# Gate units as 512-column pairs, with another release of sums, other slots and another last half group

## The chip, the cores and the metric

The kernel runs on one core of one Trainium2 chip. The metric is the device time of one execution in microseconds. Each comparison takes the median of several runs; the kernel before has 1409.77 us as the median of three runs (1408.69 to 1409.82).

## The reference

One decoder block with batch 1, 256 positions, width 2048, everything in float32. Cut to what matters:

```python
mod = silu(c) @ w_ada + b_ada                      # 2048 -> 6*2048: sh1, sc1, g1, sh2, sc2, g2
h = rms_norm(x, norm_mix_g) * (1 + sc1) + sh1
u, q, k, v, ga, gb = split(h @ w_in)               # 1024 | 3 x 1024 | 2048 | 2048
y_ssm = s5_branch(u, ...)                          # a scan over the positions, gelu, times sigmoid(y @ w_glu + b_glu)
y_att = moba_attention(q, k, v, rel_bias)          # 8 heads of 128, causal, bias by distance
merged = sigmoid(ga) * (y_ssm @ w_proj_ssm) + sigmoid(gb) * (y_att @ w_proj_attn)
x = x + g1 * (merged @ w_out)
h2 = rms_norm(x, norm_mlp_g) * (1 + sc2) + sh2
x = x + g2 * (square(relu(h2 @ w_ff1)) @ w_ff2)    # 2048 -> 8192 -> 2048
return rms_norm(x, norm_final_g)
```

## The kernel before

**Products.** A float32 product is made of three products of shorter numbers. Each weight tile is loaded as 128 x 1024 floats (512 KB, tile `wraw`, seven buffers) by SyncE's queue; ScalarE casts it to its high part (`whi`, L137) and VectorE subtracts that to get the low part (`wlo`, L139), four buffers each. The activations are split the same way (`ah`, `al`; `mh` in the second half). TensorE adds up whi·xh, whi·xl and wlo·xh in PSUM. There are five PSUM banks for the large products (`bank`) and three for others (`aux`). `stream` runs over the 128-row tiles of a weight column block, issues load, cast and subtraction ahead of time, and calls `step` after each tile.

**Forms of the product.** `gemm_t` (L174 to L176) keeps a block of 1024 weight columns in four banks and multiplies 128x128 weight blocks by 256 columns of activations, three matmuls a block: 16 tiles x 8 blocks x 3 = 384 for a unit. `gemm_w` (L202, L204) takes half as many weight columns and lets the high weight block meet high and low activations side by side in `ahl`, 512 columns; one matmul of 256 columns for the low part follows. The left 256 columns of a bank then hold one part of the result and the right 256 the other, which an evacuation has to add. ff1 works in this form. `gemm_n` and `gemm_h` (L232 to L234, L271 to L273) hold the activations as the stationary side and let 512 weight columns stream, three matmuls of 512.

**Stages.** In order: the modulation sums that the first norm needs; the units of w_in (u, q, k, v in `qkvu`; the gate columns 4096 in pieces, whose last adds are L986; then three full gate units at columns 5120, 6144 and 7168); projections and w_glu; w_out; the second norm; then ff1 and ff2 in eight groups of 1024 hidden columns; the final norm and the stores.

**Work beside it.** `step` pops jobs off lanes at a rate for each weight tile: a job is popped when the rate has added up to 1.
- Lane `ada`: the rest of the modulation, 176 loads of 512 KB with one multiply-and-sum on VectorE each (L327). Its rate is set by stage: R3 and then RS0, RS1, RS2 through w_in and the gates, RPA in the projections, RWO in w_out.
- Lanes `ssm` and `tab` build the tables of the scan. The table products (`cc`, `tt`, L581 to L583) end in TensorE's `rk` matmuls (L651), whose results VectorE takes in L657.
- Lane `m`: in gate unit 1 (columns 5120) and ahead of it the attention, from the unit's middle on (`to_ssm`) the scan.
- POOL's queue carries the hops of u between partitions (`hop_in`, L757, 32 transfers; `hop_out`) and the loads of the bias table `tz` (`bias_load`, L457, eight transfers).

**The attention.** For a head: scores `sco` (L705, L706), bias added from `tz` (L708, L709), maxima, exponentials (L713, L714), scaling (L716, L717), transposes `ptr` (L724) with a copy (L725), then `pav` (L732, L733) with a copy to `yatt` (L735). The probabilities and their transposes lie in `asc`, a part of the tile `ga`: blocks 8 to 13, one half for even and one for odd heads. Gate unit 1 has the blocks 8 to 15 of `ga` as its destination.

**Slots.** `slot` gives a named place in SBUF that several tiles hold one after the other; a tile waits until the holder before it is done. `T` and `S5` are two of them.

**Order.** The program is written in stages, but a scheduler orders the instructions of each engine by priorities and modelled times; `hot` and `high_priority` move work ahead.

## Time and profile before

| what | value |
|---|---|
| median of three runs | 1409.77 us |
| the profiled execution | 1411.44 us |
| its span | 1409.3 us |
| mean granted TensorE clock | 0.991 |
| TensorE busy | 1371.2 us |
| VectorE busy | 1056.0 us |
| ScalarE busy | 706.4 us |
| moved by DMA | 353.19 MB |

The page is of one execution, 1411.44 us; the 2.1 us between that and the span lie outside what the profiler dates. Matmuls are pipelined: one that the trace shows as 0.28 us long starts 0.12 us after the one before it, so their cost is read from start to start. Line numbers are those of the kernel before. In the changed kernel a line stands one lower than before between the constants and `homes`, and 24 higher from the new function on.

### The profile page before, as it was taken

The page shows a single profiled execution, that of the slowest core. Times are in us where ns is not written, and L with a number is a line of the kernel's source. Part 1 is how long each engine was busy: PE and PEld are TensorE (multiplying, and loading weights), DVE is VectorE, ACT ScalarE, POOL GpSimd, SP SyncE. Part 2 cuts the span into 40 slices and gives each one's busy share as a digit, 9 for nine tenths or more (in the row PEclk, how much of TensorE's full clock was granted, in tenths as well). Part 3 has the DMA queues.
Part 4 walks back from the last instruction along what each step waited for, and adds up shares of the span by engine and source line. Part 5 has one row for each costly group of instructions (what it writes and reads, how often), then busy time and mean ns, then how long its engine had stood idle before and what let it go on. Part 6 is the DMA issues. An engine that isn't in the chain of part 4 may idle for free.

```text
span 1409.3 us, 23394 instructions
## 1 busy us (share of the span) xinstructions
PE 1371.2 (97%) x9258; PEld 1221.7 (87%) x9258; DVE 1056.0 (75%) x1502; ACT 706.4 (50%) x937; POOL 40.9 (3%) x94
## 2 busy tenths in 40 slices
PE   7889999999999999999999999999999999999996
PEld 6789899899999999988788888888888888888885
DVE  5788989986799888978877776767676555655676
ACT  4454343366454853455655564545463544635444
POOL 1000000320000300000000000000000000000000
PEclk9999999999999999999999999999999999999998
DMA  9999987597457988887687677777767556565551
GB/s 349 373 382 363 318 293 233 159 299 241 149 186 257 316 294 297 296 335 276 229 298 269 209 262 239 254 247 268 264 220 263 186 188 195 176 203 191 183 203 60
DMA packets 113293, 353.19 MB, mean 251 GB/s; under 512 B 12080, under 2 KB 12096, under 8 KB 113056
## 3 DMA queue, kind: packets, MB, share of 16 engines
q1 hardware_dynamic: 110384, 347.13, 70.6%
q0 software_dynamic: 2800, 4.58, 1.1%
q8 instruction: 72, 1.18, 0.3%
q14 instruction: 37, 0.30, 0.1%
HBM read 347.27 MB, written 2.29 MB: 248 GB/s over the span
## 4 chain that ended last, share of the span: by engine, by line
PE 86%; DMA 6%; DVE 5%; ACT 1%; issue 1%; SPq 0%; DVEq 0%; ACTq 0%
PE pw L202 14%; PE pn L271 10%; PE pn L273 10%; PE pn L272 10%; PE pt L174 9%; PE pt L176 9%; PE pt L175 9%; PE pw L204 7%; DMA wraw<-in_w_in_dram 3%; DVE wlo L139 2%; DVE wraw L327 1%; PE pn L233 1%; PE pn L234 1%; PE pn L232 1%; DMA wraw<-in_wat_dram 1%
## 5 line engine op out<-in xcount | busy, mean ns | idle before, releaser
L137 ACT CAST whi<-wraw 128x1024 fp32r<-128x1024 f32 x443 | 461.9, 1052 | 553.5 <-PE pn L272 177.1
L139 DVE TENSOR_TENSOR wlo<-wraw,whi 128x1024 fp32r<-128x1024 f32 x443 | 538.3, 1223 | 255.8 <-ACT whi L137 252.9
L202 PE MATMUL pw<-mh,whi 128*128 128x512 f32 x896 | 311.5, 396 | 0.2 <-DVE part L1260 0.2
L174 PE MATMUL pt<-ah,whi 128*128 128x256 f32 x896 | 251.4, 288 | 7.2 <-ACT whi L137 5.1
L175 PE MATMUL pt<-ah,whi 128*128 128x256 f32 x896 | 250.3, 285 | 0.0
L204 PE MATMUL pw<-mh,wlo 128*128 128x256 f32 x896 | 243.0, 280 | 1.0 <-DVE wlo L139 1.0
L176 PE MATMUL pt<-ah,wlo 128*128 128x256 f32 x896 | 237.7, 286 | 2.8 <-DVE wlo L139 2.5
L327 DVE SCALAR_TENSOR_TENSOR wraw<-wraw,cb 128x1024 f32<-128x1024 f32 x176 | 213.6, 1220 | 0.0
L272 PE MATMUL pn<-whi,ff 128*128 128x512 f32 x512 | 199.3, 389 | 0.0
L271 PE MATMUL pn<-whi,ff 128*128 128x512 f32 x512 | 198.6, 390 | 0.0
L202 PEld LDWEIGHTS pw<-mh,whi 128*128 128x128 f32 x896 | 165.4, 188 | 36.3 <-issue 0.5
L273 PE MATMUL pn<-wlo,ff 128*128 128x512 f32 x512 | 185.4, 389 | 0.0
L174 PEld LDWEIGHTS pt<-ah,whi 128*128 128x128 f32 x896 | 172.1, 193 | 10.8 <-ACT whi L137 6.8
L204 PEld LDWEIGHTS pw<-mh,wlo 128*128 128x128 f32 x896 | 168.8, 188 | 5.5 <-DVE wlo L139 1.4
L175 PEld LDWEIGHTS pt<-ah,whi 128*128 128x128 f32 x896 | 172.6, 193 | 0.7 <-DVE ah L139 0.2
L176 PEld LDWEIGHTS pt<-ah,wlo 128*128 128x128 f32 x896 | 164.7, 193 | 4.8 <-DVE wlo L139 4.4
L271 PEld LDWEIGHTS pn<-whi,ff 128*128 128x128 f32 x512 | 96.1, 188 | 20.0 <-issue 0.2
L273 PEld LDWEIGHTS pn<-wlo,ff 128*128 128x128 f32 x512 | 96.1, 188 | 20.1
L272 PEld LDWEIGHTS pn<-whi,ff 128*128 128x128 f32 x512 | 96.1, 188 | 19.6
L1294 DVE TENSOR_TENSOR y<-y,pn 128x512 f32<-128x512 f32 x48 | 30.9, 683 | 14.8 <-PE pn L273 14.8
L271 PE MATMUL pn<-whi,mh 128*128 128x512 f32 x96 | 37.7, 392 | 0.0
L272 PE MATMUL pn<-whi,mh 128*128 128x512 f32 x96 | 37.4, 390 | 0.0
(400 smaller groups left out, 1658.1 us busy)
## 6 DMA issues: line engine op xcount, KB each, us to landing
wraw<-in_w_ff_dram SPq DMA_DIRECT2D x256, 512.0 KB, 4.7
wraw<-in_wat_dram SPq DMA_DIRECT2D x176, 512.0 KB, 5.5
wraw<-in_w_in_dram SPq DMA_DIRECT2D x128, 512.0 KB, 5.3
wraw<-in_w_out_dram SPq DMA_DIRECT2D x32, 512.0 KB, 6.3
wraw<-in_wan_dram SPq DMA_DIRECT2D x16, 512.0 KB, 8.7
wraw<-in_w_proj_attn_dram SPq DMA_DIRECT2D x16, 512.0 KB, 6.2
wraw<-in_w_proj_ssm_dram SPq DMA_DIRECT2D x16, 512.0 KB, 5.8
wraw<-in_w_glu_dram SPq DMA_DIRECT2D x8, 512.0 KB, 5.0
```

What stands on the lines that cost most here:

```text
L137: h = self.nc.scalar.copy(hi, src)
L139: s = self.nc.vector.tensor_sub(lo, src, hi.bitcast(F32))
L174: nc.tensor.matmul(o, hi[:, c], xh[:, kx, :], start=st, stop=False, skip_group_check=True)
L175: nc.tensor.matmul(o, hi[:, c], xl[:, kx, :], start=False, stop=False, skip_group_check=True)
L176: self.mm = nc.tensor.matmul(o, lo[:, c], xh[:, kx, :], start=False, stop=sp, skip_group_check=True)
L202: nc.tensor.matmul(banks[b], hi[:, c], x2[:, k0 + k].rearrange("p h s -> p (h s)"), start=i + k == 0, stop=False, skip_group_check=True)
L204: self.mm = nc.tensor.matmul(banks[b][:, 0:S], lo[:, c], x2[:, k0 + k, 0, :], start=False, stop=i == n - 1 and k == 1, skip_group_check=True)
L271: nc.tensor.matmul(o, xh[:, kx, tk], hi[:, c], start=q == 0, stop=False)
L272: nc.tensor.matmul(o, xl[:, kx, tk], hi[:, c], start=False, stop=False)
L273: self.mm = last = nc.tensor.matmul(o, xh[:, kx, tk], lo[:, c], start=False, stop=q == n - 1)
L327: v.scalar_tensor_tensor(w, w, 1.0, self.cb[:, (i % 2) * 1024:(i % 2 + 1) * 1024], op0=OP.mult, op1=OP.mult, accum_out=pc[:, i:i + 1])
L1294: v.tensor_add(d, d, banks[b])
```

## The change

- The three full gate units are done by `gemm_w`, in two halves of 512 columns each, with `ahl`. After each half, four times: ScalarE copies one 256-column part of a bank, and VectorE adds the other. The attention's lane is flushed when the first half of unit 1 has been issued, ahead of that half's evacuation.
- R3 goes from .5 to .25 and RS1 from .25 to .1; RPA from .65 to .85 and RWO from .45 to .65. All 176 sums are still made.
- `bias_load` stands ahead of `hop_in`. `tz`, `sri` and `yl` move from slot T to S5; `yatt` and `sg` from S5 to T.
- The second column half of the last ff2 group is done by the new `gemm_e`: row block 0 of the output while the eight tiles stream in, then row block 1 from the tiles held, as one piece of 512 columns and two of 256. Four of the tiles are held in the slot `AHL`. The final norm of row block 0 is issued between the two. Two of the four stores of row block 1 are issued by ScalarE's queue.

```diff
-R3 = .5
+R3 = .25
...
-RS1 = .25
+RS1 = .1
...
-RPA = .65
-RWO = .45
+RPA = .85
+RWO = .65
...
-TF = 3
...
-            n = 2 if tag in ("VT", "QT") else 1
+            n = {"VT": 2, "QT": 2, "AHL": 4}.get(tag, 1)
...
+    def gemm_e(self, src, kts, c0, xh, xl, homes, koff):
+        nc = self.nc
+        n = len(kts)
+        def dot(o, t, c, i, kt, hi, lo):
+            tk, kx = slice(t * P, (t + 1) * P), kt - koff
+            nc.tensor.matmul(o, xh[:, kx, tk], hi[:, c], start=i == 0, stop=False)
+            nc.tensor.matmul(o, xl[:, kx, tk], hi[:, c], start=False, stop=False)
+            self.mm = nc.tensor.matmul(o, xh[:, kx, tk], lo[:, c], start=False, stop=i == n - 1)
+        first = [(self.bank("pe0"), slice(0, 512)), (self.aux("pe1"), slice(512, 1024))]
+        held = []
+        for i, unit in enumerate(self.stream(src, kts, c0, homes)):
+            held.append((i,) + unit)
+            for o, c in first:
+                dot(o, 0, c, *held[-1])
+        yield first
+        then = []
+        for name, c in (("pe2", slice(0, 512)), ("pe3", slice(512, 768)), ("pe4", slice(768, 1024))):
+            o = (self.aux(name) if name == "pe3" else self.bank(name))[:, 0:c.stop - c.start]
+            for u in held:
+                dot(o, 1, c, *u)
+            then.append((o, c))
+        yield then
...
     def bias_load(self):
-        self.tz = self.slot("T", [P, H, S], name="tz")
+        self.tz = self.slot("S5", [P, H, S], name="tz")
...
-        self.sri = self.slot("T", [P, 2, 2, 512], name="sri")
+        self.sri = self.slot("S5", [P, 2, 2, 512], name="sri")
...
-        self.hop_in()
         self.flush("ssm")
...
+        self.hop_in()
...
-        self.yatt = self.slot("S5", [P, 8, S], name="yatt")
+        self.yatt = self.slot("T", [P, 8, S], name="yatt")
         gb = self.slot("S1", [P, KT, S], name="gb")
...
             dst, c0 = ((ga, 4096), (ga, 5120), (gb, 6144), (gb, 7168))[i]
-            banks = self.gemm_t(win, range(KT), c0, self.ah, self.al, mid=to_ssm if i == 1 else None)
-            for b in range(4):
-                nc.scalar.copy(dst[:, (i % 2) * 8 + 2 * b:(i % 2) * 8 + 2 * b + 2, :],
-                               banks[b].rearrange("p (k s) -> p k s", s=S))
+            for half in range(2):
+                banks = self.gemm_w(win, range(KT), c0 + 512 * half, self.ahl)
+                if (i, half) == (1, 0):
+                    to_ssm()
+                for b in range(4):
+                    d = dst[:, (i % 2) * 8 + 4 * half + b]
+                    with self.hot():
+                        nc.scalar.copy(d, banks[b][:, S:2 * S])
+                        v.tensor_add(d, d, banks[b][:, 0:S])
...
-        yl = self.slot("T", [P, 8, S], F32R, name="yl")
+        yl = self.slot("S5", [P, 8, S], F32R, name="yl")
...
-        sg = self.slot("S5", [P, 4, 2, S], name="sg")
+        sg = self.slot("T", [P, 4, 2, S], name="sg")
...
-        fq = self.col("fq", 8)
+        fq = self.col("fq", 9)
...
         def final(t):
...
-                v.reduce_sum(fs, fq[:, 4 * t:4 * t + 4], axis=AX.X)
+                v.reduce_sum(fs, fq[:, 4 * t:4 * t + 4 + t], axis=AX.X)
...
                 for c in (2, 0, 3, 1):
...
-                    nc.sync.dma_start(self.out[0, t * P:(t + 1) * P, cc], o)
+                    q = nc.sync if t == 0 or c in (0, 2) else nc.scalar
+                    q.dma_start(self.out[0, t * P:(t + 1) * P, cc], o)
+        def last2(t, o, c, q, keep=None):
+            keep = keep or (lambda ins: ins)
+            d = acc[:, t, c]
+            with self.hot():
+                keep(v.tensor_mul(d, o, g2b[:, c]))
+                keep(v.tensor_add(x1[:, t, c], x1[:, t, c], d))
+                nc.scalar.activation(d, x1[:, t, c], AF.Square, accum_out=fq[:, q:q + 1])
...
         def ff2(g):
             f = ffs.pop(g)
-            for cg in range(2):
-                banks = self.gemm_n(w2, range(8 * g, 8 * g + 8), cg * 1024, f[:, 0], f[:, 1], koff=8 * g,
-                                    tail=TF if g == 7 and cg else 1)
+            for cg in range(1 if g == 7 else 2):
+                banks = self.gemm_n(w2, range(8 * g, 8 * g + 8), cg * 1024, f[:, 0], f[:, 1], koff=8 * g)
...
-                        with self.hot():
-                            v.tensor_mul(d, banks[b], g2b[:, c])
-                            v.tensor_add(x1[:, t, c], x1[:, t, c], d)
-                            nc.scalar.activation(d, x1[:, t, c], AF.Square,
-                                                 accum_out=fq[:, t * 4 + cg * 2 + b % 2:t * 4 + cg * 2 + b % 2 + 1])
-                        if cg == 0:
-                            v.tensor_mul(x1[:, t, c], x1[:, t, c], gfb[:, c])
-                        elif b % 2:
-                            final(t)
+                        last2(t, banks[b], c, t * 4 + b % 2)
+                        v.tensor_mul(x1[:, t, c], x1[:, t, c], gfb[:, c])
+            if g == 7:
+                halves = self.gemm_e(w2, range(56, 64), 1024, f[:, 0], f[:, 1], self.homes(4, ("AHL",)), 56)
+                for t in range(2):
+                    for j, (o, c) in enumerate(next(halves)):
+                        last2(t, o, slice(1024 + c.start, 1024 + c.stop), t * 4 + 2 + j, self.pin if t else None)
+                    final(t)
```

**TensorE, first half of gate unit 1 and the boundary behind it.** `pt` and `pw` are the banks of gate units (`pt` by gemm_t, `pw` by gemm_w; pw_3369 to pw_3372 are the first half's four banks, pw_3754 the first bank of the second half), `pav`, `sco` and `ptr` the attention. Before, at a head late in unit 1:

```order
L174 MATMUL pt_3398<-ah,whi 128x256
L175 MATMUL pt_3398<-ah,whi 128x256
L176 MATMUL pt_3398<-ah,wlo 128x256
L732 MATMUL pav<-ga,v 128x256
L733 MATMUL pav<-ga,v 128x128
L705 MATMUL sco<-qk 128x128
L706 MATMUL sco<-qk 128x256
L724 MATMUL ptr<-ident,ga 128x128 x3
L174 MATMUL pt_3398<-ah,whi 128x256
L175 MATMUL pt_3398<-ah,whi 128x256
L176 MATMUL pt_3398<-ah,wlo 128x256
L174 MATMUL pt_3399<-ah,whi 128x256
```

After, where heads 3 to 6 stand:

```order
L201 MATMUL pw_3754<-ah,whi 128x512
L203 MATMUL pw_3754<-ah,wlo 128x256
L756 MATMUL pav<-ga,v 128x256
L757 MATMUL pav<-ga,v 128x128
L729 MATMUL sco<-qk 128x128
L730 MATMUL sco<-qk 128x256
L748 MATMUL ptr<-ident,ga 128x128 x3
L756 MATMUL pav<-ga,v 128x256
L757 MATMUL pav<-ga,v 128x128
L729 MATMUL sco<-qk 128x128
L730 MATMUL sco<-qk 128x256
L748 MATMUL ptr<-ident,ga 128x128 x3
```

Before, the heads had two dozen gate matmuls between them; now `pav`, `sco` and `ptr` of several heads follow one another.

**ScalarE at the same place.** Copies from the banks into `ga` are L1093 before and L1122 after. Before:

```order
L716 ACTIVATE ga<-ga,ast 128x128
L717 ACTIVATE ga<-ga,ast 128x256
L725 COPY ga<-ptr 128x384
L137 CAST whi<-wraw 128x1024
L1093 COPY ga<-pt_3399 128x512
L1093 COPY ga<-pt_3396 128x512
L735 COPY yatt<-pav 128x256
L1093 COPY ga<-pt_3397 128x512
L725 COPY ga<-ptr 128x384
L735 COPY yatt<-pav 128x256
L1093 COPY ga<-pt_3398 128x512
```

After:

```order
L740 ACTIVATE ga<-ga,ast 128x128
L741 ACTIVATE ga<-ga,ast 128x256
L1122 COPY ga<-pw_3369 128x256
L737 ACTIVATE ga,ast<-ga,ast 128x128
L749 COPY ga<-ptr 128x384
L738 ACTIVATE ga,ast<-ga,ast 128x256
L740 ACTIVATE ga<-ga,ast 128x128
L741 ACTIVATE ga<-ga,ast 128x256
L1122 COPY ga<-pw_3370 128x256
L1122 COPY ga<-pw_3371 128x256
L759 COPY yatt<-pav 128x256
L1122 COPY ga<-pw_3372 128x256
```

The first bank's copy of the changed kernel stands between the scalings of the heads (L740, L741), the next ones behind the last scaling.

**VectorE ahead of the last write of cc**, which the rk matmuls need. L986 (after: L1010) is the last add of the gate columns 4096, L583 (L607) the writes of the table product, L327 (L351) a sum. Before, the rows from the last L986 to the first writes of cc:

```order
L986 TENSOR_TENSOR ga<-gp,pt_2306 128x512
L139 TENSOR_TENSOR wlo<-wraw,whi 128x1024
L327 SCALAR_TENSOR_TENSOR wraw,pc<-wraw,cb 128x1024
L888 TENSOR_TENSOR A_114<-pcs,cols 128x4
L582 TENSOR_TENSOR tt<-bp,AB 128x1024
L583 TENSOR_TENSOR tt<-bp,AB 128x1024
L139 TENSOR_TENSOR wlo<-wraw,whi 128x1024
L889 SCALAR_TENSOR_TENSOR A_114<-A_114,cols 128x4
L583 TENSOR_TENSOR bp<-tt 128x32x32
L581 TENSOR_TENSOR tt<-cc,AB 128x512 x2
L139 TENSOR_TENSOR wlo<-wraw,whi 128x1024
L327 SCALAR_TENSOR_TENSOR wraw,pc<-wraw,cb 128x1024
```

After, from the last L1010 to the last write of cc:

```order
L1010 TENSOR_TENSOR ga<-gp,pt_2300 128x512
L138 TENSOR_TENSOR wlo<-wraw,whi 128x1024
L351 SCALAR_TENSOR_TENSOR wraw,pc<-wraw,cb 128x1024
L606 TENSOR_TENSOR cc<-tt 128x32x16
L138 TENSOR_TENSOR wlo<-wraw,whi 128x1024
L606 TENSOR_TENSOR tt<-cc,AB 128x512
L607 TENSOR_TENSOR tt<-cc,AB 128x512
L607 TENSOR_TENSOR cc<-tt 128x32x16
L605 TENSOR_TENSOR tt<-cc,AB 128x1024 x2
L138 TENSOR_TENSOR wlo<-wraw,whi 128x1024
L606 TENSOR_TENSOR cc<-tt 128x32x32
L606 TENSOR_TENSOR tt<-cc,AB 128x1024
```

Two sums before and one after stand between the two; the products with bp (L582, L583) that stood behind the last gate add are now ahead of it.

## The prediction

> **What bounds the kernel now.** I read the page first: busy shares, the granted clock and the shares of the chain that ended last.
>
> ```profile
> PE 1371.2 (97%) x9258; PEld 1221.7 (87%) x9258; DVE 1056.0 (75%) x1502; ACT 706.4 (50%) x937; POOL 40.9 (3%) x94
> ...
> PEclk9999999999999999999999999999999999999998
> ...
> PE 86%; DMA 6%; DVE 5%; ACT 1%; issue 1%; SPq 0%; DVEq 0%; ACTq 0%
> ...
> L139 DVE TENSOR_TENSOR wlo<-wraw,whi 128x1024 fp32r<-128x1024 f32 x443 | 538.3, 1223 | 255.8 <-ACT whi L137 252.9
> ...
> L327 DVE SCALAR_TENSOR_TENSOR wraw<-wraw,cb 128x1024 f32<-128x1024 f32 x176 | 213.6, 1220 | 0.0
> ```
>
> TensorE is busy in 97% of the span and holds 86% of the chain. A change pays only if it takes away matmul time, one of TensorE's few idle stretches, or time behind the last matmul. VectorE's two costliest groups are the lo split (1.22 us a tile) and the modulation sum (176 of 1.22 us); each sum also needs its own 512 KB load. Next came busy time by stage: gate units beside the attention (332 to 382), the later gate units (to 477), projections and w_out (to 680), the first ff1 units (to 787).
>
> ```profile
> 332.00:382.00 50.00, 50.00 (x498) 48.97 (x497) 31.67 (x58) 28.40 (x59) 0.00 (x0) 1.00 0.50 157
> 382.00:477.00 95.00, 95.00 (x1163) 93.60 (x1162) 90.30 (x125) 52.90 (x66) 12.34 (x26) 1.00 0.69 228
> 477.00:680.00 203.00, 201.83 (x1360) 186.94 (x1358) 171.08 (x228) 104.71 (x129) 3.04 (x7) 1.00 0.84 306
> ```
>
> The columns are length, then busy time of PE, weight load, DVE, ACT and POOL, clock, DMA share and GB/s. In the gate units TensorE never stops and the clock is full, so matmul time saved there is saved at the end. From 382 to 477 VectorE is busy for 90.30 of 95 us, from 477 to 680 for 171.08 of 203 with the DMA engines at 0.84: that stage has little room.
>
> **The gate units.** The start-to-start spacing of matmuls, first in a gate unit, then in an ff1 unit, which already has the form that the change gives to the gates:
>
> ```profile
> 384.72 0.28 PE L175 MATMUL pt<-ah,whi 128*128 128x256 f32 x1
> ...
> 385.92 0.28 PE L176 MATMUL pt<-ah,wlo 128*128 128x256 f32 x1
> ```
>
> ```profile
> 1266.67 0.40 PE L202 MATMUL pw<-mh,whi 128*128 128x512 f32 x1
> ...
> 1309.69 0.40 PE L202 MATMUL pw<-mh,whi 128*128 128x512 f32 x1
> ```
>
> ```profile
> 1267.00:1310.00 43.00, 42.77 (x124) 22.85 (x124) 1.00 0.58 189
> ```
>
> Ten starts take 1.20 us in the gate: 0.120 for 256 columns, 0.360 for a triple. In ff1 the 512-column matmuls (124 records in that window, the last row, counted for L202 alone) go from 1266.67 to 1309.69: 43.02/123 = 0.350 for a pair of 512 and 256 columns. A unit has 128 triples or pairs: 46.1 us now, 44.8 after, −1.3 each and **−3.9 us** for three. The Trainium skill, page "TensorE: Matmul & The Clock Gate", section "Back-to-back issue gap", gives N/2.4 + 2.5 ns as the isolated gap: 327.5 for the triple, 325 for the pair, −1.0 us in all; the measured 0.120 is not its 0.109, so I keep the rows, and its result stands among the rivals.
>
> The evacuation changes too: now four ScalarE copies of 512 columns a unit, after it eight copies of 256 and eight VectorE adds, as ff1 has them.
>
> ```profile
> L1259 ACT COPY fr<-pw x32: 359/370/376, 1021.0 to 1312.1; 128x256 f32<-128x256 f32 x32
> L1260 DVE TENSOR_TENSOR fr<-fr,pw x32: 411/414/417, 1023.4 to 1313.4; 128x256 f32<-128x256 f32 x32
> L1093 ACT COPY ga<-pt x4: 581/589/606, 363.4 to 369.7; 128x512 f32<-128x512 f32 x4
> ```
>
> ScalarE gains work of 8 × 0.37 − 4 × 0.59 = 0.6 us a unit, hidden in its half-idle time. VectorE gains 24 × 0.414 = 9.9 us; four or five sums (5 to 6 us) leave the same stage, so the net is some +4.5 us against the 23 that are free from 332 to 477. I take 0; if that cover were gone, at most those 4.5 us.
>
> **The early sums.** Fewer are released before the scan tables' first matmuls (rk). What that clears is TensorE's longest stop after the start:
>
> ```profile
> 236.02 0.69 DVE L986 TENSOR_TENSOR ga<-gp,pt 128x512 f32<-128x512 f32 x1
> ...
> 255.54 0.28 PE L175 MATMUL pt<-ah,whi 128*128 128x256 f32 x1
> ...
> 257.16 1.22 DVE L583 TENSOR_TENSOR cc<-tt 128x1024 f32<-128x1024 f32 x1
> ...
> 258.42 1.66 ACT L641 COPY tt<-cmp 128x512 f32<-128x512 f32 x3 [6.15 <-DVE cc L583]
> 259.09 0.48 PE L651 MATMUL rk<-cc,tt 64*64 64x64 f32 x4 [3.27 <-ACT tt L641]
> ```
>
> TensorE's last matmul before the stop starts at 255.54; the next waits 3.27 us for copies that wait for the last write of cc. VectorE needs 22.4 us from the last add at 236.02 to the end of that write (258.38). In the changed order there stand four lo splits, one sum and about 10 us of table work, some 16 us: 6.4 earlier, more than the stop is long. Rk keeps its place among the matmuls. The clock behind it:
>
> ```profile
> 254.68:258.09 3.41, 1.14 (x10) 0.94 (x8) 3.34 (x4) 0.00 (x0) 0.00 (x0) 1.00 0.00 0
> 258.09:264.92 6.83, 5.83 (x94) 5.49 (x96) 6.05 (x9) 4.26 (x7) 0.00 (x0) 0.50 0.57 176
> ```
>
> After the idle stretch the granted clock was 0.50 for 6.83 us. At half speed that costs at most half, 3.4 us; about 1 us of it was idle, so I estimate 2.7. Stop and clock: **−6.1 us**. Ends: 0 (something else ends the wait) and −6.7. What is late next is the lo split that feeds the following unit, which also comes earlier.
>
> The sums reappear later: by the order, 58 instead of 43 stand in the stage from 477 to 680. VectorE's 171.1 us become 171.1 + 15 × 1.22 = 189.4 of 203 (93%), and 15 more loads of 0.5 MB on 62 MB raise the DMA share of 0.84 to about 0.94. On average it fits; local pile-ups in 14 us of slack I put at **+1.0 us**. Ends: 0 and +9 (half of the 18.3 us uncovered). Behind 680 the order has 5 instead of 8 sums up to the first lo part of ff1, where TensorE waits now:
>
> ```profile
> PE pw L204 <- DVE wlo L139: 1.0, 1, 1.0
> ```
>
> This wait goes: **−0.9 us** (0 to −1.0).
>
> **Bias table and slots.** The eight loads of the bias table go ahead of the 32 hops of u on POOL's queue, which means that POOL issues them before the gather instead of behind it.
>
> ```profile
> L457 POOL DMA_DIRECT2D tz<-scr x8: 532/532/556, 288.4 to 293.1; - x8
> ```
>
> They take 8 × 0.53 = 4.3 us of that queue, and I take 0: the slot comes free with the scan tables, ahead of the hops, so they fit in front. If they didn't, u and the scan behind it would come up to 4.3 us later, under gate matmuls that fill TensorE. The attention moves up by one unit.
>
> **A new wait at unit 1's middle.** The attention's scratch lies in ga, blocks 8 to 13. Before, unit 1 (c0 = 5120) wrote ga behind the whole unit, when the heads were done. Now its first half is evacuated into blocks 8 to 11 after half a unit, so those copies wait for the heads; and with five banks the second half has one bank until then. The changed TensorE order shows it: heads 3 to 6 stand with almost no gate matmuls between them. One head now:
>
> ```profile
> 326.80 0.60 PE L706 MATMUL sco<-qk 128*128 128x256 f32 x2
> ...
> 327.23 0.49 PE L724 MATMUL ptr<-ident,ga 128*128 128x128 f32 x3
> ...
> 327.76 0.48 ACT L725 COPY ga<-ptr 128x384 f32<-128x384 f32 x1 [0.61 <-PE ptr L724]
> ...
> 329.31 0.40 ACT L713 ACTIVATE ga<-ga,ast 128x128 f32<-128x128 f32 x1
> 329.62 0.19 ACT L713 ACTIVATION_READ_ACCUMULATOR ga<-ga,ast 128x1 f32 x1
> 329.71 0.50 ACT L714 ACTIVATE ga<-ga,ast 128x256 f32<-128x256 f32 x1
> ...
> 331.08 0.49 ACT L717 ACTIVATE ga<-ga,ast 128x256 f32<-128x256 f32 x1
> 331.48 0.35 ACT L735 COPY yatt<-pav 128x256 f32<-128x256 f32 x1
> ```
>
> The loop of one head: scaling on ScalarE (0.3 + 0.5 with overlap), transposes on TensorE (0.49), copy (0.48), the next head's exponentials (0.4 + 0.5 and their read-outs, about 1.0), the output copy (0.35): 0.8 + 0.49 + 0.48 + 1.0 + 0.35 = 3.1, with hand-overs 3.2 us. The stretch has three and a half such loops, about 11.1 us, and holds by the rows above some 5.8 us of matmuls (about 1.6 a head and a few gate pairs): 5.3 idle, and 0.8 more until the last copy frees a bank. **+6.1 us.** Ends: +3 (loops overlap better) and +10 (the clock drops as well). VectorE and ScalarE go on meanwhile, but they can't bank the time: the weight buffers are four deep.
>
> **The new end.** The last half group of ff2 (eight weight tiles) is done row block 0 first, and then row block 1, whose last columns are a 256-wide piece. One bank's pass costs 3 × 8 matmuls; the extra split costs 48 × 0.118 − 24 × 0.2265 = +0.23 us by the spacing above, and perhaps 0.3 of waiting for a lo part. Behind the last matmul now:
>
> ```profile
> 1397.94 0.39 PE L273 MATMUL pn<-wlo,ff 128*128 128x512 f32 x1
> ...
> 1401.06 4.50 SPq L1281 DMA_DIRECT2D out_dram<-x  x8
> 1401.61 0.15 DVE L1272 TENSOR_REDUCE fs<-fq 128x1 f32<-128x4 f32 x1
> ...
> 1402.99 1.41 DVE L1280 SCALAR_TENSOR_TENSOR x<-x,r31s,gfb 128x512 f32<-128x512 f32 x2
> ```
>
> The reduction at 1401.61 stands behind row block 0's scaling, and all eight stores are issued on one queue until 1405.56. With row block 0 gone, the 256-wide tail (add, square) ends near 1399.9, the root takes 1.4, the two scalings 1.4, and four stores on two queues end near 1403.5: −2.1, and with the +0.5 above **−1.6 us** (−0.5 to −2.5).
>
> **Sum.** −3.9 − 6.1 + 1.0 − 0.9 + 6.1 − 1.6 = −5.4 us. The profiled execution took 1411.44 us (span 1409.3 and 2.1 around it), 1.7 above the median of 1409.77; from the median the forecast is 1409.8 − 5.4 = 1404.4, I say 1404.5. Less than 0.2% (2.8 us, 1407.0 to 1412.6) can't be told from no change.
>
> **The rivals.**
> - *A: the clock halves in the attention stretch.* That the clock falls without one long gap is seen here:
>
> ```profile
> 155.69:159.10 3.41, 1.97 (x10) 1.09 (x8) 2.56 (x5) 0.93 (x1) 0.00 (x0) 1.00 1.02 410
> 159.10:165.93 6.83, 5.27 (x24) 5.28 (x25) 6.83 (x10) 3.14 (x3) 0.00 (x0) 0.50 0.91 326
> ```
>
> ```profile
> 742.80:753.00 10.20, 9.16 (x53) 7.80 (x52) 7.47 (x12) 3.39 (x5) 0.00 (x0) 1.00 0.92 323
> ```
>
> 1.44 us idle out of 3.41, in pieces, and 0.50 for the next 6.83 us. The new stretch idles 5.3 of 11.1, some 1.6 per 3.41, just there. Price about +4: 1408.5. Against it: the last row, from 742.80 on, has 1.04 us idle in its first third and full clock to its end. The Trainium skill, page "TensorE: Matmul & The Clock Gate", section "Why this matters for your kernels", asks for no idle gap above some 3 us; by that rule no single gap here is long enough and the clock stays, which the rows above contradict, so they weigh more. Chance 0.22.
> - *B, slower: VectorE and the loads become the bound between 477 and 680.* 93% busy leaves 14 us, and TensorE needs each lo part in time. It decides once more than 6 of the 18.3 us are uncovered; half uncovered gives +9 in place of +1: 1412.5 to 1413.5. For it: the DMA share of 0.84. Against: TensorE lost only 1.2 us in these 203. Chance 0.12.
> - *C: no wait at unit 1's middle*, because the heads, which start earlier, are done when the half ends. 6.1 less: 1398.4. Against it: the order itself. Chance 0.10.
> - *D: the gap formula of the page is right for the gates*, the pair saving 1.0 instead of 3.9: 1407.4. Both spacings were measured directly. Chance 0.04.
> - *E: the change doesn't clear rk's stop*, because the copies behind it wait for something else: 6.1 more, 1410.6. Chance 0.07.
>
> **How the numbers follow.** My own case has 0.45, with 1401 to 1408. Faster: its 0.41, 0.07 of A, C's 0.10, 0.01 of D: 0.59. Same: 0.04, 0.14 of A, 0.02 of B, 0.03 of D, 0.06 of E: 0.29. Slower: 0.01 of A, 0.10 of B, 0.01 of E: 0.12. The range reaches from a little under C to B's price: 1397 to 1413.
>
> **What would show it.** In the changed profile: gate pairs 0.350 apart; no idle time before rk and a clock of 1.00 at 255 to 265; idle time of 4 to 7 us among ptr, pav and sco while the half's copies into ga wait, with the clock there telling my case from A; VectorE near 93% in the projections, with TensorE waiting for lo parts if B holds; a last store some 1.5 us sooner after the last matmul. I am wrong if the attention stretch costs much less or more than 6 us, or if a new wait shows up that the order did not let me see.

## The result and the profile after

The changed kernel is slower: median 1419.28 us of five runs (1416.18 to 1424.90) against 1409.71 of five of the kernel before, a ratio of 1.0074 with a 95% interval of 1.0061 to 1.0088. The profiled execution took 1416.18 us (span 1414.4), the shortest of the five; compared with the profiled one before it is 4.7 us longer.

The page of the changed kernel, first busy time, then the clock, then the chain that ended last:

```profile
PE 1372.6 (97%) x8898; PEld 1201.3 (85%) x8898; DVE 1064.5 (75%) x1528; ACT 707.2 (50%) x952; POOL 40.7 (3%) x94
...
PEclk9999999999999999999999999999999999999999
...
PE 87%; DVE 5%; DMA 4%; ACT 2%; issue 1%; SPq 0%; DVEq 0%; ACTq 0%
```

Nothing in the totals shows 10 us. TensorE's waits, by line, do (us in all, how often, the longest). Rk is gone from the list. Trh (the transposes behind w_out's norm) waits 5.3 us where it was 1.2. Two waits in the attention's stretch are new (pav and pw). Among the waits for casts, one of 1.8 us at w_out's first tile (pn) and one of 1.3 us early in the projections (pt) are new. First trh before, then after:

```profile
PE trh L1199 <- DVE xs L1181: 1.2, 1, 1.2
```

```profile
PE trh L1228 <- DVE xs L1210: 5.3, 1, 5.3
PE pn L295 <- ACT whi L136: 4.6, 4, 1.8
PE pt L173 <- ACT whi L136: 3.7, 4, 1.3
...
PE pav L756 <- ACT ga L749: 1.4, 2, 0.9
PE pw L201 <- DVE ga L1123: 1.2, 2, 0.8
```

The best view was the program cut at the same matmuls in each kernel. Each number is the time between two first (or last) starts in the trace, in us; the kernels below the second row are the experiments.

| kernel | start to last qkvu matmul | gates, to first proj_attn | to first proj_ssm | to first trh | to first ff1 | ff1's stages | to last matmul | behind it |
|---|---|---|---|---|---|---|---|---|
| before | 305.1 | 172.8 | 69.2 | 132.1 | 27.8 | 604.0 | 87.0 | 11.4 |
| changed | 296.9 | 177.2 | 70.9 | 140.0 | 29.9 | 602.1 | 87.5 | 10.1 |
| late_back | 299.3 | 177.3 | 69.1 | 133.3 | 29.4 | 611.2 | 87.5 | 9.8 |
| rates_back | 304.0 | 180.6 | 69.5 | 132.1 | 27.8 | 604.0 | 87.5 | 9.8 |
| rates_alone | 303.2 | 173.1 | 69.6 | 139.5 | 30.5 | 602.2 | 87.0 | 11.9 |
| gates_alone | 303.5 | 179.5 | 69.5 | 131.5 | 27.8 | 603.9 | 87.0 | 11.6 |
| end_alone | 302.4 | 173.1 | 69.2 | 131.9 | 27.8 | 604.0 | 87.5 | 9.7 |
| slots_alone | 303.6 | 172.2 | 69.2 | 131.8 | 27.8 | 603.9 | 87.0 | 11.4 |
| dve_light | 301.1 | 177.2 | 69.2 | 136.5 | 29.8 | 602.1 | 87.5 | 10.0 |
| dma_light | 300.8 | 177.3 | 69.8 | 138.2 | 29.4 | 602.1 | 87.4 | 10.0 |
| both_light | 299.7 | 177.1 | 69.1 | 135.2 | 27.6 | 602.2 | 87.5 | 10.0 |
| unit1_t | 299.8 | 174.2 | 70.6 | 138.6 | 29.1 | 602.1 | 87.4 | 10.0 |
| no_conflict | 300.8 | 175.9 | 70.3 | 140.7 | 30.1 | 602.1 | 87.5 | 10.1 |
| no_conflict_light | 299.5 | 173.5 | 69.4 | 139.6 | 30.6 | 602.1 | 87.5 | 10.1 |
| adds_light | 300.3 | 176.4 | 71.9 | 140.0 | 30.1 | 602.1 | 87.4 | 10.0 |
| end_r3 | 301.7 | 178.5 | 69.8 | 133.5 | 27.8 | 604.6 | 87.5 | 9.7 |
| end_r3b | 298.6 | 174.0 | 69.1 | 132.0 | 27.8 | 609.2 | 87.5 | 9.7 |

The first column varies between kernels that are alike there: by 2.7 us among the five with the old R3, by 4.2 us among the nine that have the changed kernel's program up to there. One cause is that the clock drops near 20, 40, 70 and 160 us fall differently in each execution: ahead of 200 us the clock is halved for 3.4 us in the changed kernel's trace and for 17.0 us in dve_light's. The other columns repeat within about 1 us where the kernels are alike. The changed kernel's gates take 4.4 us more, and the stretch from the first proj_attn to the first ff1 matmul 240.7 us in place of 229.2: 11.5 more. Ahead of them 8.2 us are gained, in ff1 and at the end 1.9 and 0.9 net. The 8.2 are partly the luck of this trace, which is of the shortest run: as a mean over kernels the gain is 3.6 (below). With 3.6 the columns add up to a loss of 9.8 us, which fits the 9.6 between the medians.

**Before rk.** The stop is gone, and the clock behind it is full:

```profile
250.00:256.00 6.00, 6.00 (x109) 5.67 (x109) 4.80 (x7) 2.99 (x6) 0.00 (x0) 1.00 0.64 215
256.00:265.00 9.00, 9.00 (x212) 8.73 (x208) 8.82 (x17) 3.05 (x5) 5.22 (x10) 1.00 0.74 143
```

**The attention.** 25 us of it in busy time by engine, before and after:

```profile
330.00:355.00 25.00, 25.00 (x199) 24.42 (x198) 14.76 (x33) 16.43 (x41) 0.00 (x0) 1.00 0.51 163
```

```profile
325.00:350.00 25.00, 21.95 (x174) 17.45 (x173) 11.18 (x30) 16.23 (x45) 0.00 (x0) 1.00 0.11 30
```

TensorE idles 3 us by this view. By start-to-start spacing about 6.5 of the 25 us are lost: the 27 gate pairs in it need 9.4 us at 0.35, the small matmuls 9.1 at the spacing they have before. The loads fall to a share of 0.11: the gate matmuls that would free weight buffers don't run. The clock stays at 1.00.

**Projections and w_out.** Each kernel from its first proj_attn matmul to the first trh, before and after:

```profile
477.80:679.20 201.40, 200.23 (x1345) 185.34 (x1343) 169.48 (x226) 103.34 (x128) 2.65 (x6) 1.00 0.84 307
```

```profile
474.10:684.90 210.80, 202.41 (x1344) 186.90 (x1342) 185.91 (x262) 101.49 (x127) 1.64 (x4) 0.99 0.91 329
```

VectorE has 16.4 us more work and the loads a share of 0.91 of a longer stretch. By their start times, 53 sums instead of 39 stand in these two stretches, and 58 instead of 44 up to the first ff1 matmul.

Some 11 of the 11.5 us are lost at three places. Early in the projections TensorE stops for 1.3 us for a late cast. At w_out's first tile it stops for 1.8 us for another, and behind that the clock is halved for 3.4 us, which costs some 1.7 more; the row from that tile on shows it as a mean clock of 0.98:

```profile
589.30:659.10 69.80, 69.76 (x321) 58.52 (x322) 61.26 (x83) 31.39 (x39) 0.00 (x0) 0.98 0.91 337
```

The rest, 4.1 us of longer wait and 2.1 behind it, is at trh, at the end of w_out; first before (SyncE starts the loads of ff1), then after (ScalarE waits for w_out's tiles between the sums' loads, and SyncE starts ff1's loads 4.9 us later):

```profile
665.83 15.14 SPq L132 DMA_DIRECT2D wraw<-in_w_ff_dram  x8
```

```profile
668.34 1.05 ACT L136 CAST wSV<-wraw 128x1024 fp32r<-128x1024 f32 x1 [1.50 <-DMA wraw<-in_w_out_dram]
...
670.68 8.76 SPq L131 DMA_DIRECT2D wraw<-in_w_ff_dram  x7
...
672.17 1.06 ACT L136 CAST wRT<-wraw 128x1024 fp32r<-128x1024 f32 x1 [1.50 <-DMA wraw<-in_w_out_dram]
...
675.33 1.05 ACT L136 CAST wS<-wraw 128x1024 fp32r<-128x1024 f32 x1 [2.11 <-DMA wraw<-in_w_out_dram]
...
679.02 0.62 PE L233 MATMUL pn<-wS,mh 128*128 128x512 f32 x2
...
679.45 0.69 DVE L1197 TENSOR_TENSOR xs<-pn,g1b 128x512 f32<-128x512 f32 x1 [0.37 <-PE pn L233]
...
684.38 0.88 DVE L1210 TENSOR_SCALAR xs<-x,r20s 128x512 f32<-128x512 f32 x2
...
684.92 1.33 PE L1228 MATMUL trh<-ident,xs 128*128 128x128 f32 x5 [5.28 <-DVE xs L1210]
```

In w_out's second half TensorE does row block 0 first and keeps row block 1's matmuls of nine tiles as cover for the norm of row block 0 (L1197 to L1210, some 5 us). Before, 21 of them stood directly ahead of trh. In the changed order the tiles come late, the kept matmuls fill the time between tiles, and none is left ahead of trh: the norm lies bare. This order is set when the program is built: from 659.1 us to the wait for trh TensorE doesn't stop, so the kept matmuls were not used up by chance, they stand earlier in the order. From 682.5, within the stop, the clock is halved for 6.8 us:

```profile
682.50:689.30 6.80, 4.38 (x15) 3.80 (x16) 5.88 (x12) 5.60 (x11) 0.00 (x0) 0.50 0.34 106
```

**The end.** The reduction of row block 1 now follows 1.8 us behind the last matmul (3.7 before), and two of its stores leave by ScalarE's queue:

```profile
1404.36 0.28 PE L260 MATMUL pe<-wAHL,ff 128*128 128x256 f32 x1
...
1406.17 0.16 DVE L1301 TENSOR_REDUCE fs<-fq 128x1 f32<-128x5 f32 x1 [0.58 <-ACT y L1319]
...
1408.93 0.88 ACTq L1311 DMA_DIRECT2D out_dram<-x  x2
```

### The profile page after: what moved, and what is told of

It is laid out like the page before. It is cut to its first block, busy times and chain, and to the rows that moved or that the text cites. A ratio compares the mean times of both kernels' runs of the same rounds, so it can differ in the third digit from the quotient of the medians.

```text
span 1414.4 us, 22726 instructions
## 1 busy us (share of the span) xinstructions
PE 1372.6 (97%) x8898; PEld 1201.3 (85%) x8898; DVE 1064.5 (75%) x1528; ACT 707.2 (50%) x952; POOL 40.7 (3%) x94
## 3 DMA queue, kind: packets, MB, share of 16 engines
q1 hardware_dynamic: 116240, 346.61, 70.6%
## 4 chain that ended last, share of the span: by engine, by line
PE 87%; DVE 5%; DMA 4%; ACT 2%; issue 1%; SPq 0%; DVEq 0%; ACTq 0%
PE pw L201 21%; PE pw L203 10%; PE pn L295 10%; PE pn L297 10%; PE pn L296 10%; PE pt L173 5%; PE pt L175 5%; PE pt L174 5%; PE pn L231 2%; PE pn L232 2%; PE pn L233 2%; DVE wraw L351 2%; DMA wraw<-in_w_in_dram 1%; DVE wlo L138 1%; DMA wraw<-in_wat_dram 1%
## 5 line engine op out<-in xcount | busy, mean ns | idle before, releaser
L351 DVE SCALAR_TENSOR_TENSOR wraw<-wraw,cb 128x1024 f32<-128x1024 f32 x176 | 213.2, 1217 | 0.0
L296 PE MATMUL pn<-whi,ff 128*128 128x512 f32 x480 | 186.9, 389 | 0.0
L295 PE MATMUL pn<-whi,ff 128*128 128x512 f32 x480 | 186.0, 390 | 0.0
L297 PE MATMUL pn<-wlo,ff 128*128 128x512 f32 x480 | 173.2, 390 | 0.0
L203 PEld LDWEIGHTS pw<-mh,wlo 128*128 128x128 f32 x896 | 168.9, 189 | 3.6
L173 PE MATMUL pt<-ah,whi 128*128 128x256 f32 x512 | 141.4, 287 | 4.9 <-ACT whi L136 2.4
L174 PE MATMUL pt<-ah,whi 128*128 128x256 f32 x512 | 141.3, 285 | 0.0
L201 PE MATMUL pw<-ah,whi 128*128 128x512 f32 x384 | 138.4, 403 | 1.2 <-DVE ga L1123 1.2
L175 PE MATMUL pt<-ah,wlo 128*128 128x256 f32 x512 | 130.3, 287 | 3.4 <-DVE wlo L138 3.3
L203 PE MATMUL pw<-ah,wlo 128*128 128x256 f32 x384 | 107.6, 282 | 0.0
L295 PEld LDWEIGHTS pn<-whi,ff 128*128 128x128 f32 x480 | 90.1, 188 | 18.9 <-issue 0.2
L296 PEld LDWEIGHTS pn<-whi,ff 128*128 128x128 f32 x480 | 90.1, 188 | 18.5
L173 PEld LDWEIGHTS pt<-ah,whi 128*128 128x128 f32 x512 | 97.8, 192 | 8.2 <-ACT whi L136 3.7
L174 PEld LDWEIGHTS pt<-ah,whi 128*128 128x128 f32 x512 | 98.8, 193 | 0.6 <-DVE ah L138 0.4
L175 PEld LDWEIGHTS pt<-ah,wlo 128*128 128x128 f32 x512 | 91.8, 193 | 5.1 <-DVE wlo L138 4.9
L201 PEld LDWEIGHTS pw<-ah,whi 128*128 128x128 f32 x384 | 71.9, 188 | 18.8 <-DVE ga L1123 1.7
```

The costliest lines, as they stand in the source:

```text
L173: nc.tensor.matmul(o, hi[:, c], xh[:, kx, :], start=st, stop=False, skip_group_check=True)
L174: nc.tensor.matmul(o, hi[:, c], xl[:, kx, :], start=False, stop=False, skip_group_check=True)
L175: self.mm = nc.tensor.matmul(o, lo[:, c], xh[:, kx, :], start=False, stop=sp, skip_group_check=True)
L201: nc.tensor.matmul(banks[b], hi[:, c], x2[:, k0 + k].rearrange("p h s -> p (h s)"), start=i + k == 0, stop=False, skip_group_check=True)
L203: self.mm = nc.tensor.matmul(banks[b][:, 0:S], lo[:, c], x2[:, k0 + k, 0, :], start=False, stop=i == n - 1 and k == 1, skip_group_check=True)
L295: nc.tensor.matmul(o, xh[:, kx, tk], hi[:, c], start=q == 0, stop=False)
```

## The experiments

Each time is a median; each ratio is against the kernel before on the same chip, with its interval.

**Rates.** late_back undoes two lines of the change, rates_back two more, and rates_alone puts the four into the kernel before.

```diff
-RPA = .85
-RWO = .65
+RPA = .65
+RWO = .45
```

> The changed kernel with RPA .65 and RWO .45 as before, R3 and RS1 as changed. Theory T (the sums moved into projections and w_out make VectorE or the loads late there): in the changed kernel's trace the stretch from the first proj_attn matmul (474.1) to the first ff1 matmul (714.8) takes 240.7 us against 229.2 before, so 11.5 us go: about 1407.8, and rk's stop stays away. Rival G (the gate units in the new form leave the splits late, and the sums only fill gaps): 1418 to 1421, as the changed kernel (1419.3). If the sums pile up in ff1 instead, in between, with new waits there.

1418.49 us, 1.0075 (1.0059 to 1.0090). The time is rival G's number, but the trace shows another cause, the pile-up in ff1 that was named last, and dearer than "in between": the stretch to the first ff1 matmul is short again (231.8), and ff1's stages take 9.1 us more than in the changed kernel, with new waits at 779 us and half the clock behind them. From 680 to 850 stand 31 sums where the changed kernel has 19.

```profile
781.00:789.00 8.00, 6.54 (x20) 5.10 (x21) 7.10 (x14) 5.04 (x5) 0.00 (x0) 0.57 1.04 395
```

> The changed kernel with all four rates of before. Theory T: the projections' 11.5 us go and the 8.2 us that the changed kernel gained ahead of the gates come back: 1416. Rival G: only the 8.2 come back: 1427.

1416.77 us, 1.0061 (1.0045 to 1.0077): theory T's number. The stretch is 229.5, the stop before rk is back, and the gates are longer still (180.6).

> The kernel before with the four rates of the change and nothing else. Theory T: some 5.5 to 8 us are gained ahead of the gates (no stop before rk) and some 11.5 lost from projections to the first ff1 matmul, by loads and VectorE: 1412 to 1415. Rival (the loss needs the new gate form, which left VectorE and the splits late): 1402 to 1404.

1414.82 us, 1.0035 (1.0023 to 1.0048). The trace is of the longest of the six runs (1418.66). Without any other edit the stretch grows to 239.6, and trh waits as in the changed kernel:

```profile
PE trh L1199 <- DVE xs L1181: 6.0, 1, 6.0
...
PE pn L271 <- ACT whi L137: 5.4, 5, 1.7
```

**What of a sum costs.** Three kernels shorten the sums between projections and w_out's end in the changed kernel; what they leave out is in the expectations.

```diff
+                m = 64 if self.cheap else 1024
-                v.scalar_tensor_tensor(w, w, 1.0, self.cb[:, (i % 2) * 1024:(i % 2 + 1) * 1024], ...)
+                v.scalar_tensor_tensor(w[:, 0:m], w[:, 0:m], 1.0, self.cb[:, (i % 2) * 1024:(i % 2) * 1024 + m], ...)
```

> The changed kernel; the modulation sums from the projections' start to w_out's end multiply and add 64 of 1024 columns (their loads stay whole), so VectorE loses some 58 sums of 1.22 us there, 65 us. If VectorE is what made that stretch long: at least 11.5 us go, 1400 to 1408. If the loads did: 1416 to 1420.

1413.80 us, 1.0037 (1.0022 to 1.0051): 5.5 us less than the changed kernel, between the two numbers. VectorE falls to 137 us of 208, and trh still waits 5.4 us, with the loads at 0.92; what goes are the stops early in the projections and at w_out's first tile.

```profile
477.00:685.00 208.00, 202.63 (x1356) 187.40 (x1355) 137.08 (x264) 104.00 (x129) 2.96 (x7) 0.99 0.92 336
```

```diff
-                ld = nc.sync.dma_start(w, self.a["wat"][r0:r0 + P, (i % 2) * 1024:(i % 2 + 1) * 1024])
+                ld = nc.sync.dma_start(w[:, 0:m], self.a["wat"][r0:r0 + P, (i % 2) * 1024:(i % 2) * 1024 + m])
```

> The changed kernel; the same sums load 64 of 1024 columns and multiply a whole tile that is in place, so VectorE works as before and some 27 MB of loads go from that stretch. If the loads made it long: 1400 to 1408. If VectorE did: 1416 to 1420. If each needs the other, both kernels gain a part.

1414.80 us, 1.0049 (1.0033 to 1.0065): 4.5 us less. Trh waits 2.3 us, and a matmul of w_out 2.7 for a cast at 651.

> The changed kernel; from the projections' start to w_out's end the sums load 64 of 1024 columns and multiply 64. Theory T (the sums' loads and their VectorE time are each enough to hold w_out up): the stretch from the first proj_attn to the first ff1 matmul, 240.7 us in the changed kernel and 229.2 before, is 229 or less, and the time 1408 to 1410. Rival (something else in the changed order, with sums only filling time): 235 and more, as with one of the two made light (235.5 and 237.4), 1413.

1407.87 us, 0.9987 (0.9977 to 0.9996): 11.4 us less than the changed kernel. The stretch is 231.9, 8.8 us shorter; the two kernels above shorten it by 5.2 and 3.3, 8.5 together. Trh doesn't wait for the norm any more. So the sums' loads and their VectorE time each carry a part of the loss, and the rival (235 and more) fails. Theory T holds for the cause; its "each enough" was too strong, and its 229 was 3 us too low.

**Gate units.** gates_alone puts only the hunk with `gemm_w` into the kernel before.

> The kernel before with the three gate units in the new form and nothing else. Theory W: the same wait, so the gate stretch is long as in the changed kernel with the old rates (180.6 against 172.75): +8, about 1417. Rival (the form saves its 3.9 us, and the loss needs the other edits): 1405.

1416.08 us, 1.0037 (1.0024 to 1.0050), near theory W's 1417. The gates take 179.5 us, 6.7 more than before, without any other edit.

```diff
+            if i == 1:
+                banks = self.gemm_t(win, range(KT), c0, self.ah, self.al, mid=to_ssm)
+                for b in range(4):
+                    nc.scalar.copy(dst[:, 8 + 2 * b:10 + 2 * b, :], banks[b].rearrange("p (k s) -> p k s", s=S))
+                continue
```

> The changed kernel with gate unit 1 (columns 5120) as before: gemm_t, evacuated behind the whole unit; units 2 and 3 in the new form. Theory W (unit 1's first half can't be evacuated while the heads use ga, and TensorE waits between heads): the stretch from the last qkvu matmul to the first proj_attn matmul, 177.2 us in the changed kernel and 172.75 before, falls by about 6.5 less the 1.3 that the unit's form saves, to 172; time about 1414. Rival V (every change between gate pairs and small matmuls costs more in the new form, in all units): 175 or more, 1417.

1416.02 us, 1.0044 (1.0030 to 1.0058). The time is near rival V's 1417, the gates lie between the two numbers: 174.2, not 172. A wait of 1.4 us for a lo part is new at 392.

```diff
-                    d = dst[:, (i % 2) * 8 + 4 * half + b]
+                    d = dst[:, b if (i, half) == (1, 0) else (i % 2) * 8 + 4 * half + b]
```

> The changed kernel; the first half of gate unit 1 is evacuated into blocks 0 to 3 of ga, which are done by then, in place of 8 to 11 (so those values are lost, and the work is the same). Theory W (copies into 8 to 11 wait for the heads): the gate stretch, 177.2 us, falls to 170 to 171.5 (172.75 before, less 3.9 for the form, plus about 1.5 of other waits); 1413 in all. Rival V (the new form itself, between small matmuls): 175 or more, 1417 to 1419.

1418.65 us, 1.0062 (1.0049 to 1.0074): rival V's numbers, 1417 to 1419 and 175 or more. Yet the wait went as theory W has it. The heads are interleaved with gate matmuls again and TensorE is busy without a break there, which shows that the copies into blocks 8 to 11 made the wait:

```profile
330.00:355.00 25.00, 25.00 (x152) 22.06 (x151) 15.19 (x31) 16.94 (x39) 0.00 (x0) 1.00 0.55 168
```

But the stretch is only 1.3 us shorter. VectorE is full from 375 on, and TensorE waits for lo parts at 387 and 412, with half the clock for 3.4 us at 414:

```profile
400.00:425.00 25.00, 21.68 (x218) 18.61 (x214) 24.90 (x36) 10.24 (x15) 0.00 (x0) 0.93 0.45 142
```

```profile
PE pw L203 <- DVE wlo L138: 3.7, 2, 2.9
```

```diff
-                        v.tensor_add(d, d, banks[b][:, 0:S])
+                        v.tensor_add(d[:, 0:32], d[:, 0:32], banks[b][:, 0:32])
```

> As the kernel whose first half of gate unit 1 goes into blocks 0 to 3, and in addition the 24 adds of the gates' evacuation work on 32 of 256 columns (0.1 in place of 0.41 us or so): VectorE gets some 7 us back. Theory X (the adds fill VectorE from 382 to 477, where it was busy 90.3 of 95 us before, and the lo parts come late): the gate stretch, 175.9 there, falls to 170 to 172, with no wait for a lo part in it; 1414 in all. Rival V (the new form costs its time at the changes to small matmuls): 175 or more, 1418.

1414.25 us, 1.0043 (1.0028 to 1.0057). The gates take 173.5 us, 2.4 less, and the waits for lo parts shrink from 3.7 to 0.6. So the adds do make the lo parts late, as theory X has it. The stretch is 1.5 above its 170 to 172: without these 0.6 and two waits for an add (1.6) it would be some 171.3, where 3.9 less than before would be 168.9. The form saves less than forecast.

> The changed kernel with its 24 adds on 32 of 256 columns and the first half in its own place. Theory W with X (the wait for the heads stands first, and behind it VectorE has had time to catch up, so the adds cost little there): the gate stretch 176 to 177.2, 1418 to 1419. Rival (the adds alone make the stretch long): 172, 1414.

1420.44 us, 1.0077 (1.0059 to 1.0095), gates 176.4: with the wait for the heads in place the adds cost 0.8 us of this stretch, as forecast. The median is above the forecast 1418 to 1419; the stretch to the first ff1 matmul, 242.0, is 1.3 longer than in the changed kernel.

Each matmul's time to the next start, summed from the first gate matmul to the first proj_attn, parts the form from the wait. "Small" are all others there, of the attention and the scan; us:

| kernel | gate matmuls | small matmuls |
|---|---|---|
| before | 141.5 | 30.8 |
| changed | 139.6 | 37.2 |
| adds_light | 139.5 | 36.5 |
| no_conflict | 144.5 | 30.9 |
| no_conflict_light | 141.1 | 31.9 |
| unit1_t | 141.3 | 32.4 |
| gates_alone | 139.7 | 39.4 |

The wait costs 6.4 us in the changed kernel and is gone in no_conflict; there the gate matmuls take 4.9 us more, with the late lo parts and the clock behind them. The form itself saves some 1.9 us in the changed kernel, with the adds short or whole.

**The rest.**

> The kernel before with the new last half group and stores and nothing else. Theory: from the last ff1 matmul to the last matmul +0.5 us, behind it -1.4 (10.0 against 11.4 us in the traces): -0.9, about 1408. Rival (the stores' landing sets the end): no difference or +0.5.

1409.52 us, 0.9996 (0.9987 to 1.0005). In the trace +0.5 us to the last matmul and -1.7 behind it; the time can't be told from no change.

> The kernel before with bias_load ahead of hop_in and the moved slots, nothing else. The parts add up (gates +5.2, rates +4.9, end -0.6 against +10.4 in all): +0.5 to +1, about 1410. Rival (the slots free the attention to start earlier and gain by themselves): 1406.

1409.30 us, 0.9998 (0.9989 to 1.0007). The attention starts its heads some 15 us earlier (first `pav` at 311.0, 325.9 before), and the gates end where they did.

The parts by their ratios: gates +5.2, rates +4.9, end -0.6, slots -0.3, together +9.2 us against +10.4 for the whole change.

**A better version was looked for** in the early rate, R3, whose lower value gains ahead of the gates. Both kernels are the one before with the new end; the second keeps RS0 at .7:

```diff
-R3 = .5
-RS0 = .7
+R3 = .25
+RS0 = 1.2
```

> The kernel before with the new last half group, R3 = .25 and RS0 = 1.2 (.7), the other rates as before: the sums that leave the stretch ahead of rk go into gate unit 1, where VectorE was busy 31.7 of 50 us. Theory T: no stop before rk (3 to 5 us less), nothing lost in w_out (229), -0.7 at the end: 1404 to 1406. Rival (any sum that is put off costs its time again): 1409 or more.

> As the one with RS0 = 1.2, but with RS0 = .7: the sums that are put off have no place of their own and move on to the lanes' later rates and the end of w_out. Theory T: stop before rk gone, a part of it lost again later, 1406 to 1411 and 1 to 4 us above the other one. Rival (only the rates RPA and RWO make the loss): the same as the other one, 1405.

1411.71 us, 1.0016 (1.0008 to 1.0024), and 1411.52, 1.0014 (1.0005 to 1.0022): no gain, and no difference between the two, as the rival of the first (1409 or more) has it. With RS0 = 1.2 the gates take 178.5 us, with .7 ff1's stages 609.2. The stop before rk is gone in both; the sums cost their time again where they land. No version that keeps the whole computation beat the kernel before beyond its interval.

## Why the prediction was wrong

Forecast were 1404.5 us and a gain; measured were 1419.28 and a loss. One step failed outright, and two terms were mis-sized.

- **The return of the early sums, +1.0: the step that failed.** "Local pile-ups in 14 us of slack I put at +1.0", with an upper end of 9. It measured 11.5 us in the changed kernel and 10.4 in rates_alone. I had the two loads right (VectorE 93%, forecast; 88% of a longer stretch, measured; loads 0.94 and 0.91), and nearly the number of sums (14 more, where the order had shown 15), and drew the wrong conclusion from an average. What counted was three places: casts that come late early in the projections and at w_out's first tile, some 4.8 us with the halved clock, and the order at w_out's end, some 6.2. There, tiles that come a few us late use up row block 1's matmuls, the only cover of the norm, and a bare norm costs its 5 us and then half the clock. That order stood in the built program, as the heads' order did, and the working doesn't look at it. The stage from 477 on was named as the one with little room; rival B had this and 0.12.
- **The early sums, -6.1.** The stop and the halved clock before rk went as forecast. The gain up to the last qkvu matmul is 3.6 us as a mean over kernels (303.7 in the five with the old R3, 300.1 in ten with the new; end_r3 and end_r3b, left out, would not change it). One reason for less than 6.1 is that the halved clock behind the stop lasted only 3.4 us in three of the five, in place of 6.8; how much of the rest is scatter of the other clock drops stays open. The term's own parts, 3.27 and 2.7, add up to 6.0.
- **The gate units, -3.9, and the wait, +6.1.** The pair came out as read: 0.23 to 0.24 and 0.12 us by start times, 0.35 where pairs follow one another. The wait for the heads was read rightly from the order and from one head's rows, and its size too: the small matmuls take 6.4 us more. The net +2.2 forecast measured +4.4 in the changed kernel and +6.7 in gates_alone. In the changed kernel the mis-sized term is the -3.9: the gate matmuls take 1.9 us less. Their 384 pairs average 0.363 us and the triples before 0.368, so the pairs are further above their clean 0.350 than the triples above their 0.360. What holds them up was not tested. "I take 0" for VectorE's 24 adds was off by little here (0.8 by adds_light) but for a wrong reason: the 23 us of free time from 332 to 477 lie ahead of 382 almost entirely (18.3 of 50), while from 382 on 4.7 of 95 were free, and the adds of units 2 and 3 fall there. Without the wait the late lo parts show it: no_conflict_light's shorter adds give 2.4 us back.
- **Right:** the wait at ff1's first lo part went (ff1's stages -1.9, forecast -0.9), slots and bias table cost nothing, the end gave -0.9 (forecast -1.6: the last store is issued 2.2 us sooner behind the last matmul, as forecast, but the span ends 4.6 us behind that issue's end, where it was 3.7).
- **The rivals.** A fails: the attention stretch kept its clock. C fails: the wait is there. D fails as written: the pair has its 0.35. But the saving, 1.9, came out nearer to its 1.0 than to 3.9. E fails: the stop before rk is gone. B holds for the cause, VectorE and the loads. It had the loss as 9 us and as lo parts that come late; most of the 11.5 is the bare norm and late casts.

What stays open: why the five runs of the changed kernel spread over 8.7 us. Only the shortest of the five has a trace here. The mean granted clock of the longest is 0.988, the lowest of the five, and that of the shortest 0.993; but two runs near 1419 have 0.994, so the clock alone doesn't order them. Open too is why the wait costs 8.6 us in gates_alone and 6.4 in the changed kernel.

## What to carry to other kernels

Work that is moved to fill free time must be placed against the free time of that very stretch, not against a stage's average: the 23 us that were to hide the adds lay in the wrong half, and the 14 that were to hide the sums did not help at the three places where a tile was needed at once. Where a schedule keeps matmuls back as cover for a latency chain, look at what late tiles do to that cover, because it is spent first. And a wait that is taken away may have been the time in which another engine caught up: no_conflict took away a wait of 6.3 us and gained 1.3.

## What the runs showed of the hardware

The halved clock follows idle time with a wide scatter. After the same stop of 3.27 us before rk it lasted 6.8 us in two kernels (before and slots_alone) and 3.4 us in three (rates_back, gates_alone, end_alone). Stops of like length were followed by it or not: 1.84 us at w_out's first tile was, in the changed kernel, and 2.00 us at the same tile was not, in no_conflict. In the changed kernel's attention 3 us of idle time in 25, in pieces of at most 0.9, left the clock at 1.00. Within the stop of 5.28 us before trh it fell to 0.50 for 6.8 us; the row of the stop itself already has 0.78 as mean:

```profile
679.64:684.92 5.28, 0.00 (x0) 0.00 (x1) 3.98 (x12) 3.73 (x8) 0.00 (x0) 0.78 0.66 264
```

The Trainium skill, page "TensorE: Matmul & The Clock Gate", section "Why this matters for your kernels", asks for no idle gap above some 3 us. These runs agree in part: the clock halved at 5.28 and 3.27 us, and not behind the attention's pieces. But gaps below 3 us were not safe: it also halved behind 1.84 us in the changed kernel, 2.21 us before trh in late_back and 2.66 us in w_out in dma_light.
